# First blocks of x by halves, new orders of differential attention and router, and 320 columns for the run of eight experts

## The chip, the cores and the metric

One core of one Trainium2 chip. The metric is device time in microseconds (us) of one launch; the kernel before takes 967.19 us (median of 3 runs, 966.83 to 968.14).

## The reference

One decoder layer on 512 tokens of width 1024 (`x`), in float32, and a final RMSNorm:

```python
h = rms_norm(x, g_mix)
fq, fk, fv, f_logit, dq, dk, dv, gate_a, gate_b = split(h @ w_in)
y_a = fox_attention(fq, fk, fv, log_sigmoid(f_logit + b))      # 8 heads of 64, causal
y_b = diff_attention(rope(dq), rope(dk), dv, lam)              # 4 heads, two softmaxes each
merged = sigmoid(gate_a) * (y_a @ w_branch_a) + sigmoid(gate_b) * (norm(y_b) @ w_branch_b)
x = x + merged @ w_out
x = x + cross_attention(rms_norm(x), rms_norm(mem))            # 4 heads, 256 memory rows
hm = rms_norm(x, g_ffn)
g_sel = argmax(hm @ w_group); ids = top_2 of the 8 experts in that group
x = x + sum over the 2 experts of weight * (silu(hm @ w_gate[e]) * (hm @ w_up[e])) @ w_down[e]
return rms_norm(x, g_final)
```

There are 32 experts, each with 6 MB of weights, all of which the kernel reads.

## The kernel before

Every order of work is written out by hand: an engine's instructions run in the order in which the program gives them, and an instruction waits for the tiles that it reads and for the buffer that it overwrites. Tokens are in NT = 4 tiles of 128, the width in KD = 8 blocks of 128. Most products are made of three float32r products: each operand is split into a high part (`A.activation` with Copy, ScalarE, line 176) and a low part (`V.tensor_tensor` subtract, VectorE, line 177). PSUM is handed out by `bank(name, tag)`: tag "a" has 2 banks, "s" 4, "y" 2. A new bank waits until the last reader of the oldest one with its tag is done.

**Start (lines 318 to 375).** `x` comes transposed, one DMA per token tile (the first in two halves), into `xT`. For tile t, `h_gain` (line 326) multiplies by the norm's gain, `h_split` makes the high part `hh` and the low part `hl` in two halves of 4 blocks (q = 0, 1), and `nat_unit` multiplies tile t with the first 256 columns of the fox values (24 matmuls, bank `fv0p`). The loop emits the unit of tile t, then gain and split of tile t + 1. At t = 1 it also splits the forget-gate columns `lg` and the third half-chunk of weights (`W.split(3)`). At t = 2 `h_stat` takes the row statistics of each tile from the untransposed `x` (lines 256 to 263 and `newton`, lines 246 to 249): a Square with a sum, Ln and Exp on ScalarE and four tiny operations on VectorE for each tile, and the evacuations of the first two units (line 306), which need the statistics `rT`, stand between the tiles. Behind the loop come the forget logits `pz` (16 matmuls), four small products `pR` that spread `rT` over the partitions (line 370), the other evacuations, and the first unit of the fox queries, `fq0p`.

**Attention (from line 927).** 16 blocks of forgetting attention (`Fox`), then 8 of differential attention (`Diff`). A Diff block makes four score banks `sd` (tag "s", line 543), the soft part, a unit of projection or branch work (tag "a"), the product of the block before, `combine`, then `W.more()` (which splits the next half-chunk of weights, lines 176 and 177), the evacuation `ev()` of the unit (lines 829 and 846 on VectorE, 830 on ScalarE), a second unit, `W.more()` again, four-block transposes of both heads into two "s" banks `td`, and their copies to SBUF `pd` (line 711: the first head by VectorE, the second by ScalarE), then `ev()` of the second unit. The next block's four `sd` banks are the four "s" banks, so two of them wait for the copies `pd`.

**Router (from line 1315).** A list of steps: `R` router logits of a token tile (16 matmuls `lg`, line 1146), `L` their transposition and scaling, `z` the single steps of the choice (z2.3 is step 3 of tile 2, all small VectorE operations but step 8, which is GpSimd's), `r` ranks of the tokens in their experts (matmuls `pr` line 1231, product `rk` line 1233), `o` the one-hot columns `G` of the first four experts (line 1238), `g` gathers with it (line 1244), `H` the split of the normalized rows into `hnh` (ScalarE, line 1129) and `hnl` (VectorE, line 1130). Behind them `places` (line 1395) works out at which column each expert's tokens begin.

**Experts (from line 1614).** Experts run in pairs p = 0 to 15: 32 gate and up matmuls each (`gu`, line 1479), transposes, down products (`yd`, line 1501) and the addition to the residual (`cb`, line 1519). The weights come in pages of 1 MB (6 for an expert) by SyncE's queue (line 1269) into a ring; a page is loaded again when its last matmul is done. Experts 0 to 3 are gathered singly. The others are gathered in three runs, `RUNS = ((4, 14), (14, 22), (22, 32))`, at p = 1, 6 and 10: `run_onehot` makes columns on VectorE, `run_gather` 8 times 8 matmuls of COLS = 384 columns (`ga`, line 1446), and `windows` copies an expert's 64 columns out of them from a column number `offi`, which `places` limits to COLS - 64 = 320. Tokens whose place lies beyond are handled as overflow: `overflow` (line 1544) loops over the experts only if an expert's count, plus what the limit cut off, is over 64.

Of the kernel before, what the change touches and what calls it, by code (L numbers as in the profile page):

```python
# [40 lines left out]
def tile_hybrid_block(  # L41
# [21 lines left out]
    def work(shape, dt, name, tag="w"):  # L63
        return wk.tile(list(shape), dt, name=name, tag=tag, bufs=bufs[tag])
# [20 lines left out]
    def xt(t):  # L85
        return X[t // 2][:, t % 2]
# [20 lines left out]
    def xT(t, k0=0, n=KD):  # L107
        return XT[t // 2][:, t % 2, k0:k0 + n]
# [206 lines left out]
        gemm(o, KD, lambda k: wh[:, k, sl], lambda k: wl[:, k, sl], lambda k: hk(HH, k), lambda k: hk(HL, k))  # L315
        return lambda: evac(j, o)

    def h_split(t, qs=(0, 1)):

        sl = slice(t * P, (t + 1) * P)  # L320
        for q in qs:
            split(HH[q][:, :, sl], HL[q][:, :, sl], xT(t, 4 * q, 4))

    def h_gain(t, k0=0, n=KD):
        v = xT(t, k0, n)
        V.tensor_tensor(v, v, gm[:, k0:k0 + n, None].to_broadcast([P, n, P]), op=OP.mult)

    def h_stat(t):
        rms_stat(xt(t), f"nx{t}", out=rT[:, t:t + 1])


    warm = bank("warm", "a")
# [3 lines left out]
    W.lazy = True  # L336
    lg = c1.tile([P, KD, 16], F32R, name="lg")
    h_gain(0, 0, 4)
    h_split(0, (0,))
    W.split(1)  # L340
    h_gain(0, 4, 4)
    h_split(0, (1,))
    W.split(2)
    evs = []
    for t in range(NT):
        evs.append(nat_unit(c_fv[0], t, fv, 0, "fv0", tag="as"[t // 2]))
        if t + 1 < NT:
            h_gain(t + 1)
            h_split(t + 1)
        if t == 1:  # L350
            split(lg[:, :, 0:8], lg[:, :, 8:16], lg_r)
            W.split(3)
        if t == 2:
            h_stat(0)
            h_stat(1)
            evs.pop(0)()
            evs.pop(0)()
            h_stat(2)
            h_stat(3)
    W.lazy = False  # L360


# [296 lines left out]
    class Diff:  # L659
# [47 lines left out]
        def copy(self):  # L707
            self.pt = []
            for i in range(2):
                r = half([P, S], F32, f"pd{self.g}{self.b}{i}")  # L710
                (V.tensor_copy if i == 0 else A.copy)(r[:, 0:self.n], self.tb[i][:, 0:self.n])
                self.pt.append(r)

        def av(self):
# [212 lines left out]
    for n, it in enumerate(its):  # L927
        it.scores()
        it.soft()
        while late:  # L930
            late.pop(0)()
        fe = rows() if rows is not None else None
        ev = unit()
        if fe is not None:
            fe()
        fin2 = prev.av() if prev is not None else None
        if n == 1:
            swap_matrix()
# [12 lines left out]
        if isinstance(it, Diff):
            ev()
            while late:
                late.pop(0)()
            ev = unit()
            W.more()
        it.trans()
        if isinstance(it, Diff):
            it.copy()
            ev()  # L960
        else:
            ev()
            it.copy()
        if n == 5:
            rotary_spread()
        rows = fin
        if isinstance(it, Fox) and it.b == NT - 1 and it.pr < 3:
            Fox(it.pr + 1, 0).prep()
        if n == 15:
            YB["h"] = page([P, 4, S], F32R, "ybh")  # L970
            YB["l"] = page([P, 4, S], F32R, "ybl")
        done, prev, fin = prev, it, fin2
# [342 lines left out]
    for step in """T0 N0 U20 Q0 U21 K0 T1 N1 U30 U22 W Q1 S0 M0 K1 U23 U31 N2 T2 S1 P0 Q2 M1 U32 A0 U33 K2 T3 O0 N3 S2  # L1315
        M2 Q3 P1 X0 K3 F0 A1 S3 M3 P2 R0 O1 L0 P3 F1 z0.0 A2 X1 z0.1 z0.2 z0.3 z0.4
        z0.5 A3 z0.6 z0.7 z0.8 O2 z0.9 z0.10 z0.11 E E E E R1 z0.12 z0.13 H0 X2 F2 L1 r0 O3 o0 z1.0 z1.1 H1 z1.2 z1.3
        F3 z1.4 z1.5 R2 z1.6 z1.7 z1.8 X3 g0.0 z1.9 z1.10 L2 z1.11 z1.12 z1.13 H2 g0.1 z2.0 z2.1 r1 z2.2 R3 o1 z2.3
        z2.4 g0.2 z2.5 z2.6 z2.7 L3 z2.8 g0.3 z2.9 z3.0 z2.10 z3.1 g1.0 z2.11 z3.2 z2.12 z3.3 z2.13 H3 g1.1 z3.4 r2
        z3.5 z3.6 o2 z3.7 g1.2 z3.8 z3.9 g1.3 z3.10 z3.11 g2.0 g2.1 z3.12 z3.13 g2.2 g2.3 r3 o3""".split():  # L1320
        f, t = step[0], int(step[1]) if len(step) > 1 else 0
        if f == "U":
            out_unit(t, int(step[2]))
        elif f == "E":
            EX.load(page)
        elif f == "W":
            W.split(2 * c_co + 2)
        elif f == "z":
            route_step(t)
        elif f == "g":  # L1330
            gather0(t, int(step[3]))
        elif f == "M":
            cross_soft(t)
            cross_scale(t)
        else:
            {"N": lambda t: x_stat(t, "nc"), "F": ffn_stat, "r": ranks, "o": lambda t: onehot(0, t), "X": x_trans, "T": cross_trans, "Q": cross_q, "K": cross_qt, "S": cross_scores, "P": cross_ptrans,
             "A": cross_av, "O": cross_out, "H": ffn_split, "R": router,
             "L": router_t}[f](t)
# [56 lines left out]
    def places():  # L1395
# [12 lines left out]
        V.tensor_tensor(off, a, n, op=OP.subtract)  # L1408
        V.memset(off[:, 0:QUAD], 0.0)

        V.tensor_scalar(a, off, float(COLS - CAP), None, op0=OP.min)
        V.tensor_copy(offi, a[0:1])
        V.tensor_tensor(b, off, a, op=OP.subtract)
        for r, (i, j) in enumerate(RUNS):
# [15 lines left out]
    def run_onehot(r, t):  # L1430

        if t == 0:
            CX["G", r] = mt([P, NT, COLS], "Gr", F32R, 1)
            CX["p", r] = p = mt([P, 2, NT], "pr", bufs=1)
            V.tensor_scalar(p, pos, -2048.0 * (r + 1), None, op0=OP.add)
        p, g = CX["p", r], CX["G", r][:, t]
        V.tensor_scalar(g, col_f, p[:, 0, t:t + 1], None, op0=OP.is_equal)
        V.scalar_tensor_tensor(g, col_f, p[:, 1, t:t + 1], g.bitcast(F32), op0=OP.is_equal, op1=OP.add)

    def run_gather(r, kb):  # L1440
        if kb == 0:
            CG[0] = mt([P, KD, COLS], "CG", bufs=1)
        o = bank(f"ga{kb}", "s")[:, 0:COLS]
        for t in range(NT):
            for u in "hl":
                PE.matmul(o, CX[u, t // 2][:, t % 2, kb * P:(kb + 1) * P], CX["G", r][:, t],  # L1446
                          start=(t == 0 and u == "h"), stop=(t == NT - 1 and u == "l"))
        A.activation(CG[0][:, kb], o, AF.Copy, scale=gfc[:, kb:kb + 1])

    def windows(p):  # L1450

# [397 lines left out]
```

## Time and profile before

| | |
|---|---|
| median of 3 runs | 967.19 us |
| profiled execution | 968.59 us |
| its span, first to last instruction | 966.8 us |
| mean granted TensorE clock | 0.994 |
| TensorE matmul busy | 936.9 us (97%) |
| VectorE, ScalarE, GpSimd busy | 484.7, 314.3, 64.5 us |
| read from HBM | 243.65 MB |

A row of a timeline has start and duration in us, engine, line and operation, output <- inputs, shapes, the number merged into the row, and in brackets the idle time before it with what ended it. PE is TensorE, DVE is VectorE, ACT is ScalarE, SPq is SyncE's queue of DMAs.

### The profile page before, as it was taken

The page shows a single profiled execution, that of the slowest core. Times are in us where ns is not written, and L with a number is a line of the kernel's source. Part 1 is how long each engine was busy: PE and PEld are TensorE (multiplying, and loading weights), DVE is VectorE, ACT ScalarE, POOL GpSimd, SP SyncE. Part 2 cuts the span into 40 slices and gives each one's busy share as a digit, 9 for nine tenths or more (in the row PEclk, how much of TensorE's full clock was granted, in tenths as well). Part 3 has the DMA queues.
Part 4 walks back from the last instruction along what each step waited for, and adds up shares of the span by engine and source line. Part 5 has one row for each costly group of instructions (what it writes and reads, how often), then busy time and mean ns, then how long its engine had stood idle before and what let it go on. Part 6 is the DMA issues. An engine that isn't in the chain of part 4 may idle for free. (4 is left out here: it accounts for less than half of the span.)

```text
span 966.8 us, 13460 instructions
## 1 busy us (share of the span) xinstructions
PE 936.9 (97%) x5234; PEld 610.6 (63%) x5235; DVE 484.7 (50%) x1075; ACT 314.3 (33%) x675; POOL 64.5 (7%) x171
## 2 busy tenths in 40 slices
PE   7999999999999999999999999999999999999995
PEld 7787788787887889999743734343633436334332
DVE  6556775857665657655754333443323541243334
ACT  4444444545352445345521211111311112111114
POOL 1840000001111200000100000000000000000000
PEclk9999999999999999999999999999999999999998
DMA  8221112221132228335669989999999999999993
GB/s 320 85 70 66 58 53 66 66 87 44 66 131 87 87 87 283 128 136 233 247 243 411 389 335 420 421 420 422 420 421 421 422 421 420 422 420 421 421 414 119
DMA packets 48290, 246.65 MB, mean 255 GB/s; under 512 B 4832, under 2 KB 12256, under 8 KB 24160
## 3 DMA queue, kind: packets, MB, share of 16 engines
q1 hardware_dynamic: 48080, 245.76, 63.9%
q8 instruction: 42, 0.69, 0.3%
q14 instruction: 24, 0.20, 0.1%
q10 hardware_dynamic: 144, 0.00, 0.0%
HBM read 243.65 MB, written 2.10 MB: 254 GB/s over the span
## 5 line engine op out<-in xcount | busy, mean ns | idle before, releaser
L1479 PE MATMUL gu<-gu,xg 128*64 128x512 f32 x1024 | 223.9, 593 | 1.9 <-DMA gu<-in_w_gu_dram 1.8
L1479 PEld LDWEIGHTS gu<-gu,xg 128*64 128x64 f32 x1024 | 72.7, 137 | 146.4 <-issue 139.1
L1501 PE MATMUL yd<-dn,A 128*64 128x512 f32 x504 | 113.6, 596 | 0.0
L177 DVE TENSOR_TENSOR wl<-wr,wh 128x1024 fp32r<-128x1024 f32 (+1 forms) x66 | 78.1, 1191 | 31.9 <-ACT wh L176 31.2
L1523 DVE TENSOR_TENSOR xr<-cb,xr 128x512 f32<-128x512 f32 x120 | 74.5, 683 | 37.8 <-PE cb L1519 37.7
L1484 DVE SCALAR_TENSOR_TENSOR A<-A,gu 128x256 f32<-128x256 f32 x32 | 13.5, 421 | 157.7 <-ACT A L1483 157.7
L1501 PEld LDWEIGHTS yd<-dn,A 128*64 128x64 f32 x504 | 35.7, 137 | 67.4 <-issue 66.6
L1483 ACT ACTIVATE A<-gu 128x256 f32<-128x256 f32 x32 | 12.3, 383 | 202.2 <-PE gu L1479 202.2
L176 ACT ACTIVATE wh<-wr 128x1024 fp32r<-128x1024 f32 (+1 forms) x66 | 67.0, 1026 | 8.7 <-DVE wr L143 7.7
L1509 DVE SCALAR_TENSOR_TENSOR Y<-yd,ws,Y 128x512 fp32r<-128x512 f32 x32 | 23.9, 751 | 90.4 <-ACT Y L1508 85.6
L1519 PE MATMUL cb<-Y,ohT 128*128 128x512 f32 x240 | 65.0, 410 | 1.6 <-DVE xr L1523 0.5
L1508 ACT ACTIVATE Y<-yd,ws 128x512 fp32r<-128x512 f32 x32 | 21.9, 687 | 119.7 <-PE yd L1501 112.4
L1519 PEld LDWEIGHTS cb<-Y,ohT 128*128 128x128 f32 x240 | 42.9, 188 | 15.4 <-DVE xr L1523 4.3
L278 PE MATMUL wop<-wh,mh 128*128 128x256 f32 x128 | 36.7, 286 | 0.2 <-DVE xr L1023 0.2
L279 PE MATMUL wop<-wl,mh 128*128 128x256 f32 x128 | 36.2, 283 | 0.0
L280 PE MATMUL wop<-wh,ml 128*128 128x256 f32 x128 | 36.2, 283 | 0.0
L1446 PE MATMUL ga<-Gr,hnh 128*128 128x384 f32 x96 | 32.4, 337 | 0.0
L1446 PE MATMUL ga<-Gr,hnl 128*128 128x384 f32 x96 | 32.1, 334 | 0.0
L584 ACT ACTIVATE S<-S,bi 128x128 f32<-128x128 f32 (+3 forms) x32 | 17.8, 556 | 29.7 <-DVE bi L581 29.7
L278 PEld LDWEIGHTS wop<-wh,mh 128*128 128x128 f32 x128 | 24.5, 192 | 0.6 <-DVE xr L1023 0.4
L279 PEld LDWEIGHTS wop<-wl,mh 128*128 128x128 f32 x128 | 24.6, 192 | 0.0
L280 PEld LDWEIGHTS wop<-wh,ml 128*128 128x128 f32 x128 | 24.5, 192 | 0.0
(617 smaller groups left out, 1859.3 us busy)
## 6 DMA issues: line engine op xcount, KB each, us to landing
gu<-in_w_gu_dram SPq DMA_DIRECT2D x128, 1024.0 KB, 19.0
dn<-in_w_dn_dram SPq DMA_DIRECT2D x59, 1024.0 KB, 19.8
wr<-in_w_inp_dram SPq DMA_DIRECT2D x40, 512.0 KB, 3.6
wr<-in_w_out_dram SPq DMA_DIRECT2D x8, 512.0 KB, 5.8
dn<-in_w_dn_dram SPq DMA_DIRECT2D x6, 512.0 KB, 14.4
x<-in_x_dram SPq DMA_DIRECT2D x2, 1024.0 KB, 11.2
wr<-in_w_branch_a_dram SPq DMA_DIRECT2D x4, 512.0 KB, 3.6
wr<-in_w_branch_b_dram SPq DMA_DIRECT2D x4, 512.0 KB, 3.5
```

What stands on the lines that cost most here:

```text
L176: A.activation(hi, src, AF.Copy)
L177: V.tensor_tensor(lo, src, hi.bitcast(F32), op=OP.subtract)
L278: PE.matmul(o, lh, rh, start=first, stop=False)
L279: PE.matmul(o, lh, rl, start=False, stop=False)
L280: PE.matmul(o, ll, rh, start=False, stop=last)
L1446: PE.matmul(o, CX[u, t // 2][:, t % 2, kb * P:(kb + 1) * P], CX["G", r][:, t], start=(t == 0 and u == "h"), stop=(t == NT - 1 and u == "l"))
L1479: PE.matmul(gu[64 * f:64 * f + 64, :], xg(2 * i + j), w[:, :, j, 256 * f:256 * f + 256], start=(i + j == 0), stop=(i + j == 4))
L1501: PE.matmul(y[j][64 * a:64 * a + 64, :], hT[a][:, f % 2, f // 2], w(a, f)[:, j, f % 2], start=(f == 0), stop=(f == 3))
L1508: A.activation(yh[rows, j], y[j][rows], AF.Copy, scale=ws)
L1509: V.scalar_tensor_tensor(yl[rows, j], y[j][rows], ws, yh[rows, j].bitcast(F32), op0=OP.mult, op1=OP.subtract)
L1519: PE.matmul(banks[j], oh[:, t * P:(t + 1) * P], y[u][:, j], start=(u == 0), stop=(u == 1))
L1523: V.tensor_tensor(xs, banks[j], xs, op=OP.add)
```

## The change

- Start: gain and high part of each later tile go by halves (gain q0, high q0, gain q1, high q1, low q0, low q1) instead of gain of the whole tile, then both splits. The splits of `lg` and of the third half-chunk move behind the last tile's. The statistics of all four tiles go together: three Squares on ScalarE, the fourth sum on VectorE, one Ln, one Exp and one set of five small VectorE operations for all. No evacuation stands between them: all four come behind `pR`.
- Diff: both copies `pd` on ScalarE; the first unit's evacuation ahead of `W.more()`. Fox blocks keep their order.
- Router: `R3` ahead of `r1`, steps z2 and z3 interleaved anew, and `H3` moved from before `r2` to behind the last step z3.13.
- Experts 14 to 21: 320 instead of 384 columns (columns, gathers, evacuations, and the limit of the column number, now 256 for them). `places` has a memset and three small operations instead of one.

```diff
+WIDE = (384, 320, 384)
...
+    def h_stat():
+
+        ss, ln, r0, v, w = (tiny([P, NT], f"nx_{n}") for n in "slrvw")
+        for t in range(NT):
+            junk = work([P, D], BF, f"nx{t}_j")
+            if t < NT - 1:
+                A.activation(junk, xt(t), AF.Square, accum_out=ss[:, t:t + 1])
+            else:
+                V.tensor_tensor_reduce(junk, xt(t), xt(t), 1.0, 0.0, OP.mult, OP.add, ss[:, t:t + 1])
+        A.activation(ln, ss, AF.Ln, scale=1.0 / D, bias=epsd)
+        A.activation(r0, ln, AF.Exp, scale=-0.5)
+        V.tensor_scalar(v, ss, 1.0 / D, 1e-6, op0=OP.mult, op1=OP.add)
+        V.tensor_tensor(w, r0, v, op=OP.mult)
...
+        V.tensor_tensor(rT, r0, w, op=OP.mult)
...
     for t in range(NT):
         evs.append(nat_unit(c_fv[0], t, fv, 0, "fv0", tag="as"[t // 2]))
         if t + 1 < NT:
-            h_gain(t + 1)
-            h_split(t + 1)
-        if t == 1:
+            h_gain(t + 1, 0, 4)
+            h_hi(t + 1, 0)
+            h_gain(t + 1, 4, 4)
+            h_hi(t + 1, 1)
+            h_lo(t + 1, 0)
+            h_lo(t + 1, 1)
+        if t == NT - 2:
             split(lg[:, :, 0:8], lg[:, :, 8:16], lg_r)
             W.split(3)
-        if t == 2:
-            h_stat(0)
-            h_stat(1)
-            evs.pop(0)()
-            evs.pop(0)()
-            h_stat(2)
-            h_stat(3)
+            h_stat()
...
-                (V.tensor_copy if i == 0 else A.copy)(r[:, 0:self.n], self.tb[i][:, 0:self.n])
+                A.copy(r[:, 0:self.n], self.tb[i][:, 0:self.n])
...
-        W.more()
         if isinstance(it, Diff):
             ev()
+            W.more()
             while late:
                 late.pop(0)()
             ev = unit()
-            W.more()
+        W.more()
         it.trans()
...
-        F3 z1.4 z1.5 R2 z1.6 z1.7 z1.8 X3 g0.0 z1.9 z1.10 L2 z1.11 z1.12 z1.13 H2 g0.1 z2.0 z2.1 r1 z2.2 R3 o1 z2.3
-        z2.4 g0.2 z2.5 z2.6 z2.7 L3 z2.8 g0.3 z2.9 z3.0 z2.10 z3.1 g1.0 z2.11 z3.2 z2.12 z3.3 z2.13 H3 g1.1 z3.4 r2
-        z3.5 z3.6 o2 z3.7 g1.2 z3.8 z3.9 g1.3 z3.10 z3.11 g2.0 g2.1 z3.12 z3.13 g2.2 g2.3 r3 o3""".split():
+        F3 z1.4 z1.5 R2 z1.6 z1.7 z1.8 X3 g0.0 z1.9 z1.10 L2 z1.11 z1.12 z1.13 H2 g0.1 z2.0 z2.1 R3 z2.2 r1 z2.3 o1
+        z2.4 g0.2 z2.5 z2.6 L3 z2.7 g0.3 z2.8 z3.0 z2.9 z3.1 g1.0 z2.10 z3.2 z2.11 z3.3 z2.12 z3.4 g1.1 z2.13 z3.5
+        z3.6 r2 z3.7 z3.8 o2 g1.2 z3.9 g1.3 z3.10 z3.11 g2.0 g2.1 z3.12 z3.13 H3 g2.2 g2.3 r3 o3""".split():
...
-        V.tensor_scalar(a, off, float(COLS - CAP), None, op0=OP.min)
+        V.memset(a[:, 0:QUAD], 0.0)
+        for (i, j), n_ in zip(RUNS, WIDE):
+            V.tensor_scalar(a[:, i:j], off[:, i:j], float(n_ - CAP), None, op0=OP.min)
...
     def run_gather(r, kb):
         if kb == 0:
             CG[0] = mt([P, KD, COLS], "CG", bufs=1)
-        o = bank(f"ga{kb}", "s")[:, 0:COLS]
+        n = WIDE[r]
+        o = bank(f"ga{kb}", "s")[:, 0:n]
```

## Rows read from the trace of the kernel before

**Rows 1.** The profile's page: matmul's busy tenths, and GB/s moved by DMA, each in 40 equal slices of the span.
```profile
PE   7999999999999999999999999999999999999995
...
GB/s 320 85 70 66 58 53 66 66 87 44 66 131 87 87 87 283 128 136 233 247 243 411 389 335 420 421 420 422 420 421 421 422 421 420 422 420 421 421 414 119
```

**Rows 2.** The view of waits, TensorE's, longest first: operation and line <- what it waited for: us in total, times, longest us.
```profile
PE fv0p L278 <- ACT hh L176: 1.9, 2, 1.0
...
PE sd L543 <- DVE pd L711: 1.7, 2, 1.2
PE br L278 <- DVE g L846: 1.6, 1, 1.6
...
PE pR L370 <- DVE rT L249: 1.2, 1, 1.2
PE pr L1231 <- DVE Mb L1213: 1.1, 1, 1.1
PE ga L1244 <- DVE G L1238: 0.9, 1, 0.9
```

**Rows 3.** Timeline of the start: TensorE, then VectorE, then ScalarE.
```profile
13.09 0.39 PE L278 MATMUL fv0p<-wh,hh 128*128 128x256 f32 x1 [0.82 <-ACT hh L176]
...
13.81 0.39 PE L280 MATMUL fv0p<-wh,hl 128*128 128x256 f32 x1 [0.22 <-DVE hl L177]
...
20.89 0.39 PE L278 MATMUL fv0p<-wh,hh 128*128 128x256 f32 x1 [1.05 <-ACT hh L176]
...
24.35 0.40 PE L365 MATMUL pz<-hh,lg 128*16 128x512 f32 x1
...
28.05 0.83 PE L370 MATMUL pR<-identf,rT 128*128 128x128 f32 x6
30.10 0.49 PE L370 MATMUL pR<-identf,rT 128*128 128x128 f32 x2 [1.22 <-DVE rT L249]
30.35 0.48 PE L278 MATMUL fq0p<-hh,wh 128*128 128x512 f32 x1
...
11.15 1.22 DVE L326 TENSOR_TENSOR xT<-xT,gm 128x1024 f32<-128x1024 f32 x1
13.06 1.29 DVE L177 TENSOR_TENSOR hl<-xT,hh 128x512 fp32r<-128x512 f32 x2 [0.69 <-ACT hh L176]
...
17.81 1.23 DVE L177 TENSOR_TENSOR wl<-wr,wh 128x1024 fp32r<-128x1024 f32 x1 [0.19 <-ACT wh L176]
...
12.40 1.15 ACT L176 ACTIVATE hh<-xT 128x512 fp32r<-128x512 f32 x2 [2.06 <-DVE xT L326]
```

**Rows 4.** The view of one tile, the untransposed x, in the first 30 us: the Squares that read it, with durations in ns (least/median/most) and the times of the first and the last; its two DMAs, the same; and the time from a DMA's issue to its landing.
```profile
L256 ACT ACTIVATE nx_j<-x x4: 1041/1042/1047, 21.3 to 27.4; 128x1024 bf16<-128x1024 f32 x4
...
L208 SPq DMA_DIRECT2D x<-in_x_dram x2: 374/378/382, 6.1 to 6.8; - x2
...
DMA to landing us min/median/max: 10.3/11.2/12.1
```

**Rows 5.** Timeline of three places in differential attention: TensorE, VectorE, ScalarE.
```profile
240.73 0.32 PE L543 MATMUL sd<-dqk1h 64*128 64x128 f32 x1 [0.20 <-ACT pd L711]
242.23 0.32 PE L543 MATMUL sd<-dqk1h 64*128 64x128 f32 x1 [1.18 <-DVE pd L711]
...
253.90 0.38 PE L543 MATMUL sd<-dqk1h 64*128 64x256 f32 x1 [0.53 <-DVE pd L711]
...
293.14 0.50 PE L278 MATMUL br<-yah,wh 128*128 128x512 f32 x1 [1.58 <-DVE g L846]
...
291.27 1.22 DVE L177 TENSOR_TENSOR wl<-wr,wh 128x1024 fp32r<-128x1024 f32 x1
292.41 0.68 DVE L846 SCALAR_TENSOR_TENSOR g<-g,br 128x512 f32<-128x512 f32 x1
...
240.09 0.58 ACT L711 COPY pd<-td 128x512 f32<-128x512 f32 x1 [2.87 <-PE td L275]
```

**Rows 6.** The view of windows: stretch, its us, busy us of PE, PEld, DVE, ACT, POOL, then the granted clock, the DMA share and GB/s. First around the wait at 242 us, then the experts.
```profile
240.00:244.00 4.00, 2.63 (x22) 2.23 (x21) 3.56 (x9) 0.93 (x3) 0.00 (x0) 0.82 0.43 132
244.00:248.00 4.00, 4.00 (x17) 3.27 (x16) 2.68 (x12) 1.85 (x9) 0.00 (x0) 0.76 0.01 3
...
936.00:940.00 4.00, 3.67 (x17) 2.03 (x18) 1.24 (x3) 0.77 (x2) 0.00 (x0) 1.00 1.04 412
...
554.00:560.00 6.00, 6.00 (x30) 3.49 (x30) 2.48 (x4) 2.25 (x4) 0.00 (x0) 1.00 0.08 27
560.00:944.00 384.00, 380.04 (x1790) 166.38 (x1788) 136.11 (x258) 63.70 (x124) 0.00 (x0) 1.00 1.01 419
```

**Rows 7.** Timeline of the router's end, VectorE; and one row of the view of waits of SyncE's DMA queue, 459 to 967 us.
```profile
485.24 1.28 DVE L1130 SCALAR_TENSOR_TENSOR hnl<-xr,nf_z,hnh 128x1024 fp32r<-128x1024 f32 x1
...
487.05 0.42 DVE L1238 TENSOR_TENSOR G<-rk,slot_f 128x256 fp32r<-128x256 f32 x1
...
489.85 0.19 DVE L1233 TENSOR_TENSOR rk<-pr,Mb 128x32 f32<-128x32 f32 x1 [0.89 <-PE pr L1231]
...
SPq L1269 <- DVE hnl L1130: 10.3, 1, 10.3
```

**Rows 8.** Timeline of the experts, the last wait of TensorE for weights; and the grouped gathers of the run of eight experts (groups by form, 640 to 720 us: count | busy us, mean ns | idle before); the low parts have a group of as many.
```profile
936.33 1.08 PE L1479 MATMUL gu<-gu,xg 128*64 128x512 f32 x4 [1.85 <-DMA gu<-in_w_gu_dram]
...
L1446 PE MATMUL ga<-Gr,hnh 128*128 128x384 f32 x32 | 10.8, 337 | 0.0
```

More of the change, by code (lines that the diff above doesn't have):

```diff
@@ L316, in t_unit, with h_hi, h_lo @@
         return lambda: evac(j, o)
-    def h_split(t, qs=(0, 1)):
+    def h_hi(t, q):
+        A.activation(HH[q][:, :, t * P:(t + 1) * P], xT(t, 4 * q, 4), AF.Copy)
+    def h_lo(t, q):
         sl = slice(t * P, (t + 1) * P)
-        for q in qs:
-            split(HH[q][:, :, sl], HL[q][:, :, sl], xT(t, 4 * q, 4))
+        V.tensor_tensor(HL[q][:, :, sl], xT(t, 4 * q, 4), HH[q][:, :, sl].bitcast(F32), op=OP.subtract)
     def h_gain(t, k0=0, n=KD):
@@ L326, in h_gain @@
         V.tensor_tensor(v, v, gm[:, k0:k0 + n, None].to_broadcast([P, n, P]), op=OP.mult)
-    def h_stat(t):
-        rms_stat(xt(t), f"nx{t}", out=rT[:, t:t + 1])
+    def h_stat():
[10 more added lines that the diff above has]
+        V.tensor_tensor(w, r0, v, op=OP.mult)
+        V.tensor_tensor(w, w, r0, op=OP.mult)
+        V.tensor_scalar(w, w, -0.5, 1.5, op0=OP.mult, op1=OP.add)
+        V.tensor_tensor(rT, r0, w, op=OP.mult)
     warm = bank("warm", "a")
@@ L338, in tile_hybrid_block @@
     h_gain(0, 0, 4)
-    h_split(0, (0,))
+    h_hi(0, 0)
+    h_lo(0, 0)
     W.split(1)
     h_gain(0, 4, 4)
-    h_split(0, (1,))
+    h_hi(0, 1)
+    h_lo(0, 1)
     W.split(2)
@@ L1435, in run_onehot @@
             V.tensor_scalar(p, pos, -2048.0 * (r + 1), None, op0=OP.add)
-        p, g = CX["p", r], CX["G", r][:, t]
-        V.tensor_scalar(g, col_f, p[:, 0, t:t + 1], None, op0=OP.is_equal)
-        V.scalar_tensor_tensor(g, col_f, p[:, 1, t:t + 1], g.bitcast(F32), op0=OP.is_equal, op1=OP.add)
+        p, g = CX["p", r], CX["G", r][:, t, 0:WIDE[r]]
+        col = col_f[:, 0:WIDE[r]]
+        V.tensor_scalar(g, col, p[:, 0, t:t + 1], None, op0=OP.is_equal)
+        V.scalar_tensor_tensor(g, col, p[:, 1, t:t + 1], g.bitcast(F32), op0=OP.is_equal, op1=OP.add)
     def run_gather(r, kb):
@@ L1442, in run_gather @@
             CG[0] = mt([P, KD, COLS], "CG", bufs=1)
-        o = bank(f"ga{kb}", "s")[:, 0:COLS]
+        n = WIDE[r]
+        o = bank(f"ga{kb}", "s")[:, 0:n]
         for t in range(NT):
             for u in "hl":
-                PE.matmul(o, CX[u, t // 2][:, t % 2, kb * P:(kb + 1) * P], CX["G", r][:, t],
+                PE.matmul(o, CX[u, t // 2][:, t % 2, kb * P:(kb + 1) * P], CX["G", r][:, t, 0:n],
                           start=(t == 0 and u == "h"), stop=(t == NT - 1 and u == "l"))
-        A.activation(CG[0][:, kb], o, AF.Copy, scale=gfc[:, kb:kb + 1])
+        A.activation(CG[0][:, kb, 0:n], o, AF.Copy, scale=gfc[:, kb:kb + 1])
     def windows(p):
```

## The prediction, as put on record before the run

> **What bounds the kernel now.** I read the page first: TensorE is busy in nearly all of the span, and DMA moves little up to slice 19 and then an even 420 GB/s or so to the end [rows 1]. So there are two kernels in a row: up to about 490 us one that TensorE's work bounds, in which each idle stretch of TensorE that goes makes everything behind it earlier; and the experts, of which the windows must say whether TensorE or the weights end last. The waits of TensorE [rows 2] say which idle stretches there are; timelines around each say what ends it [rows 3, 5, 7].
>
> **The experts are bound by the weights from 560 us on.** The windows [rows 6] show DMA nearly idle from 554 to 560 us (27 GB/s): the ring is full, because TensorE is in the first run's gather and frees no page. From 560 to 944 us DMA never pauses (419 GB/s, share 1.01), and at 936.33 TensorE waits 1.85 us for a page [rows 8]. So where TensorE stands at 560 us sets when the last weights land; what TensorE saves after that comes back as a longer wait for weights.
>
> **Start, 4.0 us.** Tile 1: the gain of 1024 columns runs 11.15 to 12.37, the high part starts at 12.40, two halves in 1.15 (0.63 for the first), TensorE starts the tile at 13.09 and has its first low part at 13.81 [rows 3]. With halves the first gain ends after about 0.69 (half of a two-step row as that of `hl`, 1.29 for two), the high part at 12.50, TensorE starts at 12.55, the low part is there at 13.28: 0.53 earlier. One tile now costs VectorE four halves of about 0.62, 2.5 us, and the high part lies beside them; a tile of 24 matmuls costs TensorE 2.9 (24 starts 0.12 apart, from the pace between 13.81 and 24.35 without its waits). So tiles 2 and 3 don't wait any more. Tile 3 waited 1.05 and 0.22 because the weights' split `wl` (1.23) stood ahead of its gain [rows 3]; that split now comes after, and its first reader is `fq0p`. Stretch by stretch: from the first low part 22 + 24 + 24 matmuls at 0.12 are 8.4, so `pz` starts at 21.7 instead of 24.35, 2.7 earlier. `pz` takes 3.7 (24.35 to 28.05), `pR` 0.9, and nothing else stands between if `rT` is there at 25.4. Its chain: high parts of tile 3 until 18.3, `lg` and the third half-chunk on ScalarE until 19.4, three Squares of 1.04, the last starting at 21.5. Before, the last Square began at 27.4 and the product that needs its result at 30.10, 2.7 later [rows 3, 4]; with one small operation more I take 2.9, so 24.4, 1.0 before it is wanted. The rows of x are there: issued at 6.1 and 6.8, landed after at most 12.1, by 18.9 [rows 4]. The sum on VectorE (1024 columns, two inputs) isn't in the trace; 1.23 for `wl` is nearest, 0.7 to 2 the bounds, beside the Squares either way. `fq0p` then starts at 26.3 instead of 30.35: 4.0. If `rT` were late by 1.4 and more, only 2.7 would be left; 4.3 is the most, with every restart gone. The late evacuations of units 0 and 1 sit on ScalarE before `pR` is done, and `fq0p`'s bank is free with the first of them. GpSimd's rotary work starts when `fv0p` ends, so it too is earlier.
>
> **Diff, 3.1 us of waits.** At 242.23 TensorE has waited 1.18 for the copy `pd` on VectorE, which stands behind a weights' split and an evacuation [rows 5]; ScalarE made the other copy at 240.09 and is idle then. As a second copy on ScalarE it ends at about 241.15 (0.58 each, 0.48 apart): 1.0 earlier. At 253.90 likewise 0.53, of which 0.5 goes. The two blocks with the other long rows wait about 0.3 each in the middle of `sd`, which shows as matmuls stretched rather than idle; I take 0.5 for both. At 293.14 TensorE waited 1.58 for an evacuation at 292.41 that stood behind a split of 1.22 started at 291.27 [rows 5]. Now the evacuation goes first: 1.1 earlier. Sum 1.0 + 0.5 + 0.5 + 1.1 = 3.1. What is behind the moved steps: on ScalarE the split's high part now waits for the evacuation's VectorE step, on VectorE the low part is 0.6 later; the half-chunk split there is for the next block's unit, a soft part and four score banks away. ScalarE gets 0.3 to 0.6 a block and waits for TensorE ahead of `pd` in the rows shown (2.87 idle). From 0.6 (a later wait takes most of it) to 3.8 (no wait left).
>
> **The clock, 1.7 us.** Behind the wait at 242 us the granted clock is 0.82 and 0.76 in two windows of 4 us [rows 6]: TensorE was at the lower of its two levels (1.2 instead of 2.4 GHz) for a part of each, and lost 0.72 + 0.96 = 1.7 us there. Before it fell, TensorE had idled 0.20 and 1.18 within 1.5 us. With these gone I expect no fall. But 1.58 at 293 and 1.85 at 936 brought none (1.00 behind the latter [rows 6]), so what makes it fall isn't plain: from -1.7 (a fall elsewhere as well as here) to 1.7.
> The Trainium skill ("TensorE: Matmul & The Clock Gate", section "A second HAM failure mode: psum-queue depth-cycling") has the clock toggle where TensorE often idles briefly for PSUM. The row at 242 is of that kind, but the other waits for banks brought no fall. By that rule the sum is this one; without it, 1.7 less.
>
> **Router, 0.8 us.** TensorE's waits of 1.11 for `Mb` and 0.93 for `G` [rows 2] come from one chain of small VectorE steps; TensorE isn't what ends it. In that chain VectorE works on `hnl` of tile 3 for 1.28 from 485.24, ahead of the ranks of tile 2, and later idles 0.89 until 489.85 for the last ranks [rows 7]. `H3` behind z3.13 puts 1.2 us of work into that idle time: `G` of tile 2 is about 0.9 earlier, tile 3's choice too, `hnl` runs while TensorE does its last gathers, and the last ranks are multiplied at about 489.05. `R3` ahead of `r1` fills the first wait with 1.9 us of matmuls, at the price of a wait before `r2`, as z2.13 now stands behind z3.4. I take 0.8, from 0.2 (z2's steps, stretched by z3's, keep the end) to 1.1. `H3` also ends a wait of SyncE's queue, for `hnl` [rows 7]: that load of a page of down weights is issued some 2 us later against TensorE. It isn't read before the first pair's second half of down products, 20 us on, and the next load in the queue waits for TensorE's first gate matmuls anyway.
>
> **Experts, -0.1 us.** 64 gathers of the middle run are a sixth shorter: 32 of the high parts are 10.8 busy for 384 columns and overlap by half, so 64 take some 11, and a sixth is 1.85 [rows 8]. By the windows it is worth nothing, since it lies behind 560 us. Three more small operations in `places` (0.19 each, as `rk` [rows 7]) hide behind the first experts' matmuls; I take 0.1, 0 to 0.6.
>
> **Sum.** 4.0 + 3.1 + 1.7 + 0.8 - 0.1 = 9.5 off the profiled execution's 968.59: 959.1. Its time is 1.4 above the median of 967.19, so 957.7 is the forecast in the terms of the median.
>
> **Rivals.** (1) One fall of the clock stays or comes anew: 959.4. For it: the fall isn't explained by the wait's length, and the saved 1.85 makes the waits for weights near 936 us add up to 3.7. The Trainium skill (the same page, section "HAM oscillation — how this bites in real kernels") has such DMA waits bring the lower clock, which here would strike the last pair, where TensorE's work is followed by the output; the trace has 1.85 without a fall. (2) Diff's waits pass to another engine: only start, router and experts are left, 4.7, and 962.5. For it: VectorE is as busy as before around 242 but for one copy. (3) TensorE bounds the experts after all and the shorter gathers count: 955.9. Against it stands a DMA share of 1.01 over 384 us. (4) `rT` is late, 1.4 less: 959 to 960.5. (5) Weights set the experts' start as well, so that nothing before 560 counts: 967.2; the idle 554 to 560 us speaks against it. (6) Slower: the narrower limit sets off the overflow loop. With the reference's inputs (seed 0, its own router) experts 14 to 21 have 28, 29, 30, 35, 39, 47, 49 and 27 tokens, so the last begins at 257, one beyond the limit of 256, and counts as 28; the loop runs from 65. Were it to run, one expert's six pages of 1 MB at 419 GB/s are 15 us, with TensorE idle: 973 and up.
>
> **Chances.** Forecast 0.50; (1) 0.20; (2) 0.10; (3) 0.08; (4) 0.07; (5) 0.03; (6) 0.02. The range 955.5 to 962.0 leaves out (2), (5) and (6). A measurement of this kernel can tell 0.2%, 1.9 us, from no change: faster 0.95, same 0.03, slower 0.02.
>
> **What would show it.** Right: `fq0p` starts near 26.3; no wait of TensorE for `rT`; `sd` waits under 0.4; granted clock 1.00 from 240 to 248; DMA's pause before 560 us earlier by as much as the end; and TensorE's waits for `gu` near the end up by some 1.85. Wrong: a pause of DMA after the first gather, a new wait of `fv0p`, `br` or `pr` over 1 us, or a granted clock below 1.00 before the output.

## The result, and the profile after

The changed kernel takes 956.69 us (median of 4 runs, 956.52 to 957.53), beside 967.04 (966.83 to 968.14) for the kernel before: a ratio of 0.9894, 95% interval 0.9879 to 0.991. The forecast was 957.7, range 955.5 to 962.0. The profiled execution after took 956.52 us with a span of 954.8; the one before had 968.59 and 966.8, so the two traces differ by 12.0 us where the medians differ by 10.4. The profiled execution of before lies 1.5 above its kernel's median here, that of after 0.2 below its own.

TensorE's view of waits after the change answers to [rows 2]:

```profile
PE gu L1500 <- DMA gu<-in_w_gu_dram: 3.2, 4, 1.8
...
PE pr L1248 <- DVE Mb L1230: 1.0, 1, 1.0
PE fv0p L279 <- ACT wh L177: 0.6, 1, 0.6
...
PE br L279 <- DVE g L863: 0.5, 1, 0.5
```

The waits for `pd` (1.7) and `rT` (1.2) are gone, `hh`'s of 1.9 is 0.3 (first row below), `br`'s of 1.6 is 0.5, and the wait for weights, 1.85 before [rows 8], has become 3.2. `pr`'s of 1.1 is 1.0: it moved from the ranks of tile 1 to those of tile 2, as the prediction says, and what went is the 0.9 for `G`.

The timeline of the start, TensorE, then ScalarE, then VectorE, answers to [rows 3]:

```profile
11.53 0.38 PE L279 MATMUL fv0p<-wh,hh 128*128 128x256 f32 x1 [0.30 <-ACT hh L321]
12.26 0.39 PE L281 MATMUL fv0p<-wh,hl 128*128 128x256 f32 x1 [0.22 <-DVE hl L325]
...
20.76 0.40 PE L382 MATMUL pz<-hh,lg 128*16 128x512 f32 x1
24.46 1.05 PE L387 MATMUL pR<-identf,rT 128*128 128x128 f32 x8
25.27 0.48 PE L279 MATMUL fq0p<-hh,wh 128*128 128x512 f32 x1
...
5.00 1.14 ACT L177 ACTIVATE wh<-wr 128x512 fp32r<-128x512 f32 x2
20.36 1.04 ACT L337 ACTIVATE nx_j<-x 128x1024 bf16<-128x1024 f32 x1
...
19.55 1.22 DVE L339 CUSTOM_DVE_ANT_0 nx_j<-x 128x1024 bf16<-128x1024 f32 x1
22.74 0.16 DVE L346 TENSOR_TENSOR rT<-nx_r,nx_w 128x4 f32<-128x4 f32 x1
```

From the first low part of tile 1 at 12.26 TensorE runs without a wait to `fq0p` at 25.27. `rT` is finished at 22.90, 1.6 before `pR` wants it. `fq0p` starts 5.1 earlier than before (30.35), but the first weights' split is 1.1 earlier too: 5.00, where before had this:

```profile
6.08 1.15 ACT L176 ACTIVATE wh<-wr 128x512 fp32r<-128x512 f32 x2 [1.01 <-DMA wr<-in_w_inp_dram]
```

Their load is issued at 1.2 in both traces and lands at 4.94 and 6.06, and the loads issued ahead of it are the same. Over all fourteen traces of this case the split starts between 5.00 and 6.15. Whether that is chance is not shown: each kernel has one trace, and the seven with the new statistics have it at 5.00 to 5.63, the seven without at 5.67 to 6.15. Less this 1.1, the change brought 4.0 at the start; the five other traces with the whole new start give 4.0 to 4.1 in the same way (start only with the 1.7 of its own fall of the clock added, below).

Windows after the change answer to [rows 6]: around the block of differential attention that had the wait at 242 us (the same matmul is now at 234.88), then DMA's pause, the weights behind it, and the end.

```profile
234.00:238.00 4.00, 3.74 (x29) 2.95 (x28) 3.67 (x11) 2.14 (x9) 0.00 (x0) 1.00 0.29 87
238.00:242.00 4.00, 4.00 (x27) 3.57 (x26) 2.85 (x8) 1.71 (x10) 0.00 (x0) 1.00 0.12 48
...
541.00:549.00 8.00, 8.00 (x40) 4.72 (x41) 2.48 (x4) 2.32 (x4) 0.00 (x0) 1.00 0.27 87
549.00:934.00 385.00, 379.66 (x1794) 164.66 (x1790) 136.08 (x259) 64.27 (x126) 0.00 (x0) 1.00 1.01 418
934.00:955.00 21.00, 10.02 (x36) 4.84 (x32) 10.87 (x26) 10.74 (x26) 0.00 (x0) 0.83 0.26 100
```

The granted clock (the column behind POOL's) stays at 1.00 where it was 0.82 and 0.76. DMA's pause, which held 554 to 560 us before, now falls in 541 to 549, and behind it the weights run without a break for 385 us at 418 GB/s, as they did for 384 at 419.

The router's end, VectorE, answers to [rows 7]; below it, from the view of waits of SyncE's DMA queue:

```profile
474.07 0.19 DVE L1230 TENSOR_TENSOR Mb<-Wh,Wh 128x32 bf16<-128x32 f32 x1
...
476.37 1.28 DVE L1147 SCALAR_TENSOR_TENSOR hnl<-xr,nf_z,hnh 128x1024 fp32r<-128x1024 f32 x1
477.64 0.19 DVE L1250 TENSOR_TENSOR rk<-pr,Mb 128x32 f32<-128x32 f32 x1
477.87 0.42 DVE L1255 TENSOR_TENSOR G<-rk,slot_f 128x256 fp32r<-128x256 f32 x1
...
SPq L1286 <- DVE hnl L1147: 12.4, 1, 12.4
```

`hnl` now lies where VectorE idled 0.89 for the last ranks, and nothing stands between it, `rk` and `G`. SyncE's queue waits 2.1 longer for it (10.3 before); nobody waits for that queue, whose next load comes long before its use.

To see where the 12.0 us came from, I took the start of the same matmul in two traces and subtracted; the times at the top are those of before, and minus is earlier. The other kernels are those of the experiments.

| us, in before | 13.1 | 30.4 | 188 | 231 | 240.7 | 242.2 | 253.9 | 282.5 | 293.1 | 487.5 | 640 | 903 | 932.5 |
|---|---|---|---|---|---|---|---|---|---|---|---|---|---|
| after | -1.6 | -5.1 | -5.4 | -5.6 | -6.3 | -7.4 | -9.3 | -9.8 | -11.1 | -12.1 | -12.2 | -13.9 | -12.0 |
| start only | -0.4 | -3.1 | -3.4 | -3.4 | -3.4 | -3.4 | -5.0 | -5.0 | -5.0 | -5.0 | -5.0 | -4.9 | -5.1 |
| start, halves | -0.6 | -1.9 | -2.2 | -2.2 | -2.2 | -2.2 | -2.2 | -2.2 | -2.1 | -2.2 | -2.1 | -2.1 | -2.1 |
| start, statistics | -0.8 | -3.9 | -4.2 | -4.2 | -4.2 | -4.2 | -5.8 | -5.7 | -5.7 | -5.7 | -5.8 | -5.8 | -5.8 |
| Diff only | -0.1 | -0.4 | -0.4 | -0.7 | -1.4 | -2.4 | -4.4 | -4.9 | -6.2 | -6.2 | -6.1 | -6.1 | -6.2 |
| copy only | 0.0 | -0.3 | -0.3 | -0.6 | -1.3 | -2.4 | -4.3 | -4.9 | -5.0 | -5.0 | -5.0 | -4.9 | -4.4 |
| order only | -0.4 | -0.7 | -0.7 | -1.0 | -1.3 | -1.3 | -3.5 | -4.0 | -5.3 | -5.3 | -5.3 | -5.2 | -4.8 |
| router only | 0.1 | -0.2 | -0.3 | -0.3 | -0.3 | -0.3 | -0.3 | -0.3 | -0.3 | -1.4 | -1.4 | -1.4 | -0.6 |
| columns only | 0.0 | -0.3 | -0.3 | -0.3 | -0.3 | -0.3 | -0.3 | -0.3 | -0.3 | -0.3 | -0.3 | -2.0 | -0.3 |
| first run 256 | -1.0 | -4.6 | -4.8 | -5.0 | -5.7 | -6.8 | -8.8 | -9.3 | -10.6 | -11.7 | -15.2 | -16.9 | -15.1 |
| no low parts in run two | -1.0 | -4.5 | -4.8 | -5.1 | -5.8 | -6.8 | -8.8 | -9.4 | -10.6 | -11.7 | -11.8 | -14.0 | -12.1 |

Read along a row: each step down is a stall that went (at 13.1 also the landing of the first weights, at 253.9 mostly the fall of the clock behind 242), and a number that comes back up between 903 and 932.5 was given back to the wait for weights. In "after", 1.7 gained by the shorter gather at 903 is gone again at 932.5.

### The profile page after: what moved, and what is told of

The parts are those of the page before. It is cut to its first block, busy times and chain, and to the rows that moved or that the text cites. A ratio compares the mean times of both kernels' runs of the same rounds, so it can differ in the third digit from the quotient of the medians.

```text
span 954.8 us, 13450 instructions
## 1 busy us (share of the span) xinstructions
PE 930.9 (98%) x5234; PEld 606.1 (63%) x5235; DVE 481.2 (50%) x1064; ACT 313.8 (33%) x675; POOL 64.9 (7%) x171
## 5 line engine op out<-in xcount | busy, mean ns | idle before, releaser
L1467 PE MATMUL ga<-Gr,hnh 128*128 128x384 f32 (+1 forms) x96 | 31.1, 329 | 0.0
L1467 PE MATMUL ga<-Gr,hnl 128*128 128x384 f32 (+1 forms) x96 | 30.8, 326 | 0.0
```

## The experiments

Two theories went into the experiments. Mine: ahead of the weights' pause TensorE sets the pace and every stall that goes counts in full, behind it the weights do and nothing that TensorE saves counts; the four parts add up, and the fall of the clock belongs to the `sd` wait. The rivals: columns count, the waits of one part pass to another, or the fall has another cause. The medians of the kernel before lay between 967.6 and 967.9 in these runs, and its single times between 966.0 and 969.1.

**The parts alone.** Each is the kernel before with one part of the diff. The start:

```diff
-            h_gain(t + 1)
-            h_split(t + 1)
+            h_gain(t + 1, 0, 4); h_hi(t + 1, 0); h_gain(t + 1, 4, 4); h_hi(t + 1, 1)
+            h_lo(t + 1, 0); h_lo(t + 1, 1)
...
+            h_stat()
```

> The kernel before with the new start alone. My theory: TensorE reaches the queries' first unit 4 to 5 us earlier, no later stretch takes it back, and DMA's pause in the first run's gather comes as much earlier: 4 to 5 us faster. Rival (the weights bind the experts from 490 us on, so that nothing saved ahead of them counts): no change.

Measured: 964.04 (963.24 to 964.8), ratio 0.9966, 0.9952 to 0.998: 3.6 us, less than the 4 to 5 expected. Its profile has a surprise, in the windows (busy PE, granted clock, DMA share, GB/s):

```profile
8.00:12.00 4.00, 1.86 (x14) 1.00 1.02 416
12.00:16.00 4.00, 3.89 (x20) 0.57 1.04 415
```

The clock fell in the start, behind a wait of 1.8 for the weights' split `wh`, and cost 4 x 0.43 = 1.7 us; in exchange the fall at 242 us did not come, though the waits for `pd` there are as long as before. Without the first the start would be worth 4.8 at 30.4 us in this trace.

Differential attention, copy and order together:

```diff
-                (V.tensor_copy if i == 0 else A.copy)(r[:, 0:self.n], self.tb[i][:, 0:self.n])
+                A.copy(r[:, 0:self.n], self.tb[i][:, 0:self.n])
...
-        W.more()
         if isinstance(it, Diff):
             ev()
+            W.more()
```

> The kernel before with both copies of Diff on ScalarE and the evacuation ahead of the weights' split, and nothing else. My theory: 3.1 us of waits go, and where the execution compared had a fall of the clock at 242 us, 1.7 more: 3 to 5 us faster, and a granted clock of 1.00 from 220 to 300 us. Rival (the clock falls there for another cause than the wait): the waits go, the fall stays somewhere between 220 and 300, about 3 us or less.

Measured: 962.69 (962.51 to 963.4), ratio 0.9953, 0.9939 to 0.9966: 4.9 us, at the upper end of the 3 to 5 expected. No wait for `pd` over 0.2 is left, no fall of the clock, `br` waits 0.5, and the runs lie within 0.9 us of one another.

The router's order alone (the three changed lines of steps):

> The kernel before with the new order of the router's end alone. My theory: VectorE's chain of small steps ends the stretch, and the low part of tile 3 fills VectorE's idle 0.9: 0.8 to 1.1 us faster. Rival (the wait moves from the ranks of tile 1 to those of tile 2): within 0.2 us.

Measured: 966.67 (965.45 to 967.99), ratio 0.999, 0.9981 to 0.9999: 0.9 us. The trace has 1.1 at the router's end, and 0.8 of it given back at the weights near 932 us: their stretch, from the first page behind the pause to the last landing, took 388.4 us here and 387.2 to 388.0 in the thirteen other traces. The fall at 242 is still there in the profiled execution, which is the slowest of the eleven.

The 320 columns alone:

> The kernel before with 320 columns for the middle run alone. My theory: the weights bind from 560 us on; the middle gather takes 1.85 us less, TensorE waits 1.8 longer for weights near the end, and the time is the same within 0.3 us. Rival (TensorE binds the experts): 1.85 us faster, with no longer waits for weights.

Measured: 968.14 (966.44 to 968.45), ratio 1.0002, 0.9993 to 1.0011: nothing. The row of the table shows why: 1.7 us gained over the gather (-0.3 to -2.0), and -0.3 again at the last wait for weights.

**Copy and order apart.** First the copy alone, then the order alone.

> The kernel before, with both copies pd of differential attention on ScalarE and nothing else. By the prediction's terms 1.0 + 0.5 at the sd waits of VectorE's copy, 0.5 at the two other blocks (this may belong to the order instead), and the fall of the clock at 242, if it follows the idle time there, 1.7: 3.2 to 3.7, so 964 to 964.5 beside 967.7, with a narrow spread of the runs, as there is no fall left that some runs have and others not. Rival, the fall has another cause: 1.5 to 2.0, 965.7 to 966.2. Rival, the second copy delays ScalarE's evacuations: under 1.

Measured: 963.77 (963.72 to 964.68), ratio 0.996, 0.9947 to 0.9974: 4.2 us, a little over the 3.2 to 3.7 of the first theory. The clock is 1.00 up to the output.

> The kernel before, with the evacuation of differential attention's unit ahead of the weights' split and nothing else. By the prediction's terms 1.1 at 293 (br's wait 1.6 becomes 0.5), and at most 0.5 at 231 and 282: 966.1 to 966.6 beside 967.7; the copy's waits at 242 and 254 stay, and the fall of the clock with them. Rival, the evacuation ahead of the split also frees VectorE for the copy at 242 (it stood behind a split and an evacuation): the sd wait goes here too, and copy and order each do the same 2 to 3 us, so that their sum is more than the 4.9 of both.

Measured: 963.8 (963.25 to 965.28), ratio 0.9963, 0.9949 to 0.9977: 4.1 us, against 1.1 to 1.6 expected. The profiled execution (waits between 215 and 300 us, a row of the timeline, and two windows) has the wait and no fall:

```profile
PE sd L543 <- DVE pd L711: 1.2, 1, 1.2
PE br L278 <- DVE g L846: 0.4, 1, 0.4
...
240.90 0.32 PE L543 MATMUL sd<-dqk1h 64*128 64x128 f32 x1 [1.17 <-DVE pd L711]
...
240.00:242.00 2.00, 1.10 (x14) 1.00 0.32 88
242.00:244.00 2.00, 2.00 (x12) 1.00 0.53 182
```

The `sd` wait is still there, 1.17 instead of 1.18, with the same 0.20 ahead of it, and the clock does not fall in this execution; in two of the five executions it does, by their mean granted clock of 0.994 (the table under "Clock" below). By the table above the order brought 1.2 at 293 and some 0.45 to 0.65 at each of three other blocks (231, 253.9 and 282.5). There the rival was right: the earlier evacuation frees VectorE for the copy, though not at 242. The copy alone takes much of these same small stalls, so that 4.2 and 4.1 alone make 4.9 together.

**The start, split.** The halves alone (gain, high part, gain, high part, then the low parts, with the statistics as before), and the statistics alone (grouped and last, with whole blocks as before). The second kernel also has the splits of `lg` and of the third half-chunk behind the last tile's, as the change has; the first doesn't.

> The kernel before, with one part of the new start alone: gains, high and low parts of blocks 1 to 3 of x by halves, in the new order; the statistics, their order and the early evictions stay. If the start's gain lies in tile 1 to 3 coming earlier to TensorE: about 1.5 us where tiles 1 and 2 no longer wait for their blocks, but the wait of the broadcast of the statistics behind the logits stays (2 to 3 us of it), so 1 to 2 us of the 3.6: 965.5 to 966.6. Rival, the statistics are the last to come anyway and take all of it back: 967.6, no change. Rival, the halves carry it all and the statistics hardly anything: 964.

Measured: 965.71 (964.21 to 966.78), ratio 0.9977, 0.9968 to 0.9986: 2.0 us. As expected; of `pR`'s wait for `rT`, 0.9 stays. The fall of the clock is there in the profiled execution, 2.2 us earlier than in the kernel before, as all its work is:

```profile
240.03 0.32 PE L547 MATMUL sd<-dqk1h 64*128 64x128 f32 x1 [1.16 <-DVE pd L715]
...
240.00:242.00 2.00, 1.97 (x14) 0.64 0.70 256
242.00:244.00 2.00, 2.00 (x6) 0.51 0.00 0
```

> The kernel before, with the other part of the new start alone: the statistics of the four blocks grouped (one Ln and one Exp, the last sum on VectorE) and put behind the last block, the evacuations behind them; gains and splits of whole blocks as before. The halves alone gave 2.0 (0.9977 [0.9968, 0.9986]), the whole start 3.6. If the two add up: 1.6, 966.0 to 966.3. Rival, the wait of the broadcast for the statistics is the last thing in either case, so each alone gets more or less than its part: no change (the blocks come late, as before, and the statistics behind them) or 2.5 and more.

Measured: 963.61 (962.69 to 965.16), ratio 0.9965, 0.9951 to 0.9979: 4.3 us, where 1.6 was expected if the two add up; the rival had 2.5 and more. The profiled execution is the fastest of the five, 962.69. By its row of the table 3.9 stands at 30.4 us: 0.8 from ahead of tile 1, 1.5 at tile 3, which no longer waits behind the weights' split, and 1.4 at `pR`. So only about half of what this kernel adds belongs to the statistics. Another 1.6 comes where before had the fall of the clock. Here too the wait is there, and in this execution the fall is not:

```profile
238.00 0.32 PE L558 MATMUL sd<-dqk1h 64*128 64x128 f32 x1 [1.19 <-DVE pd L726]
...
238.00:240.00 2.00, 2.00 (x17) 1.00 0.79 252
240.00:242.00 2.00, 2.00 (x11) 1.00 0.00 0
```

**What counts ahead of the weights' pause.** The changed kernel with 256 columns for the first run too:

```diff
-WIDE = (384, 320, 384)
+WIDE = (256, 320, 384)
```

> The changed kernel, with the first of the three runs of experts at 256 columns too (384, 320, 384 become 256, 320, 384; all tokens of these inputs still fit their windows). The 64 matmuls of that gather stand ahead of the pause of the weights' DMAs (541 to 549 us), so theory one (after the pause the weights set the pace, ahead of it TensorE does) expects what they save: 128 columns of 384 at about 0.165 us a matmul, 64 x 0.055 = 3.5 us: 953.2 (952.5 to 954.5). Rival, the weights set the end from wherever they start and the pause only moves: 956.7, no change. Rival, other waits of the gather (evictions of ScalarE, the one-hot of VectorE) take the place: 955 to 956.7.

Measured: 953.5 (953.1 to 953.78), ratio to the kernel before 0.9854, 0.9841 to 0.9868, clear of the changed kernel's interval. It beats both kernels. Windows of this kernel over the two stretches of after that are shown above:

```profile
541.00:549.00 8.00, 8.00 (x39) 2.92 (x39) 2.31 (x4) 0.93 (x3) 0.00 (x0) 1.00 0.68 245
549.00:931.00 382.00, 376.72 (x1780) 163.70 (x1776) 136.13 (x259) 64.28 (x126) 0.00 (x0) 1.00 1.01 418
```

The weights resume earlier (a share of 0.68 in 541 to 549 instead of 0.27) and run on at the same 418 GB/s. In the table this kernel is 0.5 behind the changed one at 30.4 us, 0.4 behind at 487.5, 3.0 ahead at 640, and still 3.0 ahead at 932.5: the gather's 3.4 counts in full.

The same with the cut of the runs moved:

```diff
-RUNS = ((4, 14), (14, 22), (22, 32))
-WIDE = (384, 320, 384)
+RUNS = ((4, 12), (12, 22), (22, 32))
+WIDE = (256, 384, 384)
```

> The changed kernel with the cut of the runs moved: experts 4 to 11, 12 to 21 and 22 to 31, at 256, 384 and 384 columns. The first gather is 128 columns narrower (ahead of the pause), the second 64 wider (behind it). Theory one: the first counts, 64 x 0.055 = 3.5 us, and the second, 64 x 0.027 = 1.7 us, is hidden by the weights: 953.2, as with the first run at 256 alone (and not 954.9). Rival, TensorE sets the end: 3.5 - 1.7 = 1.8 us: 954.9. Rival, only the weights: 956.7. Since the second run begins two experts earlier, another gather falls closer to the pause, and a part of the 1.7 may count.

Measured: 953.72 (952.89 to 954.55), ratio 0.9856, 0.9841 to 0.9871. The first gather's 128 columns count; the second's 64 more cost nothing that can be seen, as in "columns only" they gave nothing.

**What counts behind it.** The changed kernel, with fewer matmuls in the second run's gather:

```diff
-            for u in "hl":
+            for u in ("h" if r == 1 else "hl"):
...
```

> The changed kernel, with the 32 matmuls of the low parts left out of the second run's gather (its 8 experts get tokens without their low parts): TensorE does about 32 x 0.14 = 4.5 us less, behind the pause of the weights' DMAs. Theory one (behind the pause the weights set the end): no change, 956.7 (956 to 957.4), with longer waits for the up and gate weights in the last experts: 3.2 us of them would become about 7. Rival, TensorE sets the experts' pace: 952.2 to 953.

Measured: 959.31 (957.94 to 960.89), ratio 0.9917, 0.9903 to 0.993: 2.6 slower than the changed kernel, which no theory had. The timelines of the last experts, first of after, then of this kernel:

```profile
924.29 1.94 PE L1500 MATMUL gu<-gu,xg 128*64 128x512 f32 x8 [1.82 <-DMA gu<-in_w_gu_dram]
...
935.01 1.18 PE L1714 MATMUL cl<-Y,ohT 128*128 128x512 f32 x4 [0.45 <-DVEq L1569]
```
```profile
924.23 1.94 PE L1500 MATMUL gu<-gu,xg 128*64 128x512 f32 x8 [1.84 <-DMA gu<-in_w_gu_dram]
...
936.45 1.17 PE L1714 MATMUL cl<-Y,ohT 128*128 128x512 f32 x4 [1.94 <-PEq L1569]
```

The question asked is answered by the first row of each: TensorE was 4.1 ahead behind the gather and starts the last gate and up products 0.06 ahead. All of it is lost again at gate and up products, whose waits for weights are 6.0 in this kernel and 3.2 in after. The slower end is another matter: at the branch behind the last expert (L1569, the overflow loop's) TensorE waits 1.94 for its own queue of instructions instead of 0.45. That is 1.4 of the 2.6. The profiled execution is the fastest of the five; the other 1.2 is in no trace. The three slowest executions have a mean granted clock of 0.994 to 0.995 where the profiled one has 0.996, so a fall of the clock or a longer end may be in them; which, is not on record.

To see whether the branch follows the number of instructions, the same with all 32 low matmuls kept, of 32 columns (in all three runs the last tile's low one goes ahead of its high one):

```diff
+                m = 32 if r == 1 and u == "l" else n
-                PE.matmul(o, CX[u, t // 2]..., CX["G", r][:, t, 0:n],
+                PE.matmul(o[:, 0:m], CX[u, t // 2]..., CX["G", r][:, t, 0:m],
...
```

> The changed kernel, with the low parts of the second run's gather kept for 32 of the 320 columns only (the other tokens of its 8 experts lack their low parts): as many instructions as the changed kernel has, but about 32 x 0.12 = 3.8 us less on TensorE behind the pause of the weights' DMAs. The run that left out the 32 matmuls was at its last up and gate matmul as early as the changed kernel and then lost 1.5 at the branch behind the last expert, where TensorE's instruction queue was the last to come. If that comes from the number of instructions and so from where the code of the branch lies: no such wait here, and with the weights as the bound 956.7 (956.2 to 957.2). If it comes from the shorter gather, 958 to 959 again. Rival, TensorE sets the pace behind the pause: 953.

Measured: 957.14 (956.11 to 957.25), ratio 0.9892, 0.9877 to 0.9907: as the changed kernel. From its view of waits:

```profile
PE gu L1501 <- DMA gu<-in_w_gu_dram: 3.7, 5, 1.8
...
PE cl L1715 <- DVEq L1570: 0.4, 1, 0.4
```

The wait at the branch is 0.4 again. So the longer wait came with the missing instructions; that the place of the code is what decides is my reading and was not tried. As a test of the pace, and of whether the shorter gather plays a part, this kernel says less than meant: its gather saved 1.2, not 3.8, as a high and a low matmul together still take 0.26 us instead of 0.30.

## Why the prediction was right

**What bounds it: right.** Work that TensorE is spared counts in full ahead of the weights' pause, 3.4 of 3.5 (first run 256), and not at all behind it, where 0.06 is left of 4.1 at the last gate and up products (no low parts) and 0.0 of 1.7 (columns only). The plainest sign is the weights' stretch. Behind the pause every one of the fourteen traces has 159 loads of weights, and from the issue of the first to the landing of the last pass 387.2 to 388.4 us (387.5 in before, 387.7 in after), while the first is issued anywhere from 559.0 (before) to 546.8 (after) and 543.8 (first run 256). Some 20.2 to 20.9 us follow, 21.8 only in the kernel with the long wait at the branch. "In full" holds up to the scatter of that stretch, which took 0.8 of the router's 1.1 in one trace. Rival (3), that columns count, and rival (5), that nothing ahead of the experts does, are both out. The wait for weights rose by 1.35, from 1.85 to 3.2, where I had a rise of 1.85.

**Start, 4.0: right, and by its own steps.** 5.1 in the trace less the 1.1 of the weights' landing. With that 1.1 added back, tile 1 starts at 12.6 (forecast 12.55), `pz` at 21.8 (21.7), `rT` is there at 24.0 (24.4) and `fq0p` starts at 26.4 (26.3). The sum of squares on VectorE, which no row showed, takes 1.22, as the row I had taken for it (1.23). I had not said how the parts of the start share: at 30.4 us the halves alone bring 1.8, and statistics and moved splits 3.0 (3.9 less the 0.8 from ahead of tile 1), about half of it each. That is 4.8 beside the whole start's 4.0, so about 0.8 of it is the same waiting, taken away by either.

**Diff's waits, 3.1: mechanism right, size too small.** The table's row for after falls by 5.7 from 188 to 293 us; less the clock's 1.7 that is 4.0. The two large terms came as forecast (1.1 at 242 for 1.0, 1.2 at 293 for 1.1), and 253.9 gave 0.25 for 0.5. What I under-sized is the wait in the middle of `sd`: I saw it as stretched matmuls at two blocks and took 0.5 for both. By the table it is 0.9 from 188 to 240.7 us and 0.5 at 282.5, together 1.4.

**Clock, 1.7: right, but the wait is only half of the reason.** The fall went, as forecast, and 1.7 is what it was worth. But I tied it to the 1.18 of idle time at 242, and three traces have that wait without a fall behind it: order only (1.17), statistics only (1.19) and start only, whose fall came elsewhere, at 12 us. Halves only has 1.16 and the fall. A trace is one execution. The record also has the mean granted clock of the others: it is 0.994 to 0.995 in the five traces with a fall ahead of the output and 0.996 to 0.997 in the nine without, so the executions can be counted by it.

| kernel | wait of 1.2 for `pd` | 0.996 to 0.997: executions, median us | 0.991 to 0.995: executions, median us |
|---|---|---|---|
| before, beside the experiments | yes | 15, 966.6 | 30, 968.1 |
| start only | yes | 1, 963.2 | 4, 964.2 |
| start, halves | yes | 4, 964.6 | 7, 966.3 |
| start, statistics | yes | 3, 963.3 | 2, 965.1 |
| order only | yes | 3, 963.8 | 2, 964.3 |
| router only | yes | 4, 965.7 | 7, 967.0 |
| columns only | yes | 4, 966.9 | 7, 968.2 |
| Diff only, copy only, after, first run 256, eight in the first run, 32 low columns | no | 27 | 0 |
| no low parts in run two | no | 2, 958.2 | 3, 959.7 |

With the wait the mean is low in 59 of 93 executions; in six kernels without it, in none of 27. So removing the wait did remove the fall, as the prediction has it, but the wait alone doesn't bring it, and what decides from one execution to the next stays open. A mean says that there was a fall and not where; "no low parts" is the one kernel without the wait that has low means. The Trainium skill ("TensorE: Matmul & The Clock Gate", section "A second HAM failure mode: psum-queue depth-cycling") blames frequent short waits of TensorE for PSUM; these traces agree only in that no trace without the short waits has the fall there. The falls that its section "HAM oscillation — how this bites in real kernels" led me to fear at the weights' waits, rival (1), did not come: behind waits of 0.3 and 1.8 the clock is 1.00 up to 934 us (the waits in that section are about 3 to 5 us long).

**Router, 0.8: right.** 1.1 in the trace of the changed kernel and in that of the router alone; 0.9 by the medians, with an interval that reaches from 0.1 to 1.8. Each column of the table above taken by itself gives the same, 0.9 and 1.1.

**Columns, 0: right.** The overflow loop, rival (6), did not run: at its branch TensorE idles 0.45 and goes on.

**The sum.** 4.0 + 4.0 + 1.7 + 1.1 make 10.8 of the 12.0 between the traces; 1.1 is the landing of the first weights. By medians the four parts alone give 3.6 + 4.9 + 0.9 - 0.5 = 8.9 of 10.4; where the other 1.5 lies is not shown, but four of start only's five executions still have a fall of the clock, and of the changed kernel's four none has.

**Luck in the number.** The forecast took the clock's 1.7 off the profiled execution of before, and then 1.4 more because that execution lay above the median. But it lay there in the main because it had the fall: 968.1 with one and 966.6 without are the medians in the table (the clocks of the three runs behind 967.19 are not on record). So the clock was counted nearly twice. Compared without a fall on either side, the other terms forecast 4.0 + 3.1 + 0.8 - 0.1 = 7.8, and 966.6 - 956.7 = 9.9 was measured. The 2.1 that were missing are about Diff's 0.9, the router's 0.3 and up to 1.1 of the first weights' landing, which I can't divide between chance and the change. The two errors largely cancel, and so the result is only 1.0 below the forecast.

## What to carry to other kernels

Find in the windows where DMA pauses: TensorE's savings ahead of that point count in full, behind it they turn into longer waits, so cut the work ahead of it first (here 128 columns in the first gather, 3.2 us for one number, where 64 in the second gave nothing). A stall shows as idle time or as stretched matmuls in the middle of a group; count the blocks that have it before you size it. And one trace neither proves nor disproves a cause for a fall of the granted clock: count the falls by the mean clock of every execution, and compare executions with a fall with one another and those without likewise.

## What the runs showed of the hardware

- The clock can fall or not behind the same wait at the same instruction: after 1.16 and 1.18 it fell and cost 1.7 us, after 1.17 and 1.19 it did not. Over the executions of the kernels with that wait the mean clock was low in 59 of 93, without it in none of 27, one kernel (3 of 5) aside.
- The first weights, issued at 1.2 in every trace, landed between 4.8 and 6.1 us after the span's start, and in the changed kernel's trace TensorE's whole start is 1.1 earlier by it.
- The same 159 loads of weights took 387.2 to 388.4 us in fourteen traces, wherever they began between 543.8 and 559.0.
- TensorE's queue waited 1.94 instead of 0.45 at a branch when 32 matmuls were missing ahead of it, and 0.4 when they were there but short.
